# Row factors of two RMS norms sent to all partitions through DRAM instead of by a diagonal and a matrix product

## The chip, the cores and the metric

The kernel runs on one core of a Trainium2 chip. The metric is the device time of one execution in microseconds (us). The kernel before takes 1819.01 us, the median of three runs (1817.65 to 1820.26).

## The reference, cut to what matters

The program is one hybrid decoder layer in float32 and a last norm, on 2048 tokens of 1024 features.

```python
h = rms_norm(x, norm1_g)
proj = h @ w_in                                  # u_a, v_a, val_b, gate_b
a_out = spatial_gating(u_a, v_a, ...)            # within chunks of 128 tokens
b_out = conformer_conv(val_b, gate_b, ...)       # causal depthwise, 31 taps
x = x + concat([a_out, b_out]) @ w_out
h = rms_norm(x, norm2_g)                         # the second norm
f = square(relu(h @ w_ff1))
x = x + f @ w_ff2
return rms_norm(x, final_g)                      # the last norm

def rms_norm(x, g):
    return x * rsqrt(mean(x * x, axis=-1) + EPS) * g
```

Each norm needs one factor per token, r = rsqrt(mean of squares + EPS). The two norms that matter here are the second and the last.

## The kernel before, in words

Activations lie transposed: features on the 128 partitions, tokens along the row. The 2048 tokens are four blocks (b = 0 to 3) of 512; a tile of 128x512 holds 128 features of one block. A factor per token is therefore a factor per column, and must be the same on all 128 partitions before it can multiply a tile.

**How a factor comes about.** The squares of a block are added over the eight feature tiles (square_add), and feature_sums (L490) multiplies them by a column of ones, which gives the sum over partitions as a tile of 128x4: token 128n + p stands at partition p, column n (tile ssum). VectorE (DVE) computes ve, the mean plus EPS, and GpSimd (POOL) raises it to -1/2: r, 128x4.

**How r reaches all partitions before.** DVE multiplies an identity by r, which gives dg, four diagonals of 128x128; TensorE (PE) multiplies it by a matrix of ones, so that every partition of the PSUM tile rbc holds all 512 factors. The two matrices are plain fp32, and the trace shows two records for this one product. For the second norm ScalarE (ACT) copies the tile to SBUF, into r_rows (row_scale, L625). For the last norm of blocks 0 and 1 the tile rbc3 stays in PSUM and is read from there by eight products of DVE, one for each feature tile (finish, L1129).

**Precision.** Other products are made of three matmuls (mm3) on fp32r parts: high x high, low x high and high x low. ACT makes the high part and POOL, or DVE, the low one.

**The stages.** The input projections and the convolution come first. stage_o(b) (L647) is the output projection of block b; when its last tile is done, row_scale(b) is put on a list with a due time. later(n, f) (L598) runs f at the n-th following beat, and beat comes twice for each tile. The up multiply u0 serves blocks 0 and 1, u1 blocks 2 and 3, each as seven products over 2x2 blocks in place of eight; up_out (L978) multiplies each sum by r_rows on DVE (L992, recorded as c<-c,r_rows or c<-py,r_rows) and squares it. The down multiply has 16 chunks, numbered 0 to 15, eight for each pair of blocks. A chunk (down_chunk, L1242) has 28 steps, STEPS (L1084), each named (i, j): i is one of the seven products and j one of four tiles. A step is six matmuls into a tile py and one DVE addition from it to a residual tile x. Products 1, 5 and 2 open PSUM tiles; 6, 7 and 4 go on in the four tiles of product 1, and 3 goes on in those of product 5. So a step of product 3 has to wait until the addition that reads the same tile after product 5 is done. The steps begin (1,0) to (1,3), (5,0) to (5,2), (6,0) to (6,3), (3,0) to (3,2), (5,3). In the down phase there are eight PSUM banks for all of this, ssum and rbc3 included.

**The finishes.** Blocks 1 and 0 are complete in the last steps of chunk 7. finish(b) is a generator that goes one step on at each step of chunks 8 and 9, beside the matmuls: sums, r, gaps of so many steps, diagonal, product, and then one product of DVE and one store a step. Blocks 3 and 2 end the kernel; their finishes (finish_third, finish_last) are other functions and stay as they are.

**What sets the order.** Most of the program, the down phase but its last chunk included, is reordered by the framework's scheduler, which simulates a timeline. stage_o, the two up multiplies and the last chunk keep the order as written. Engines run their instructions in order, and wait by semaphores. SyncE (SP) issues nearly all DMAs in one order, and stands still while one of them waits.

Of the kernel before, what the change touches and what calls it, by code (L numbers as in the profile page):

```python
# [9 lines left out]
F32 = mybir.dt.float32  # L10
# [3 lines left out]
ALU = mybir.AluOpType  # L14

P = 128
# [3 lines left out]
TB = 512  # L20
KD = D // P
# [6 lines left out]
V_FG = 36  # L28
# [54 lines left out]
def hybrid_block_kernel(  # L83
# [14 lines left out]
    nc = tc.nc  # L98
    dve = Clocked(nc.vector, lambda n: 0.35 if n <= 128 else 0.17 + n / 960.0)
    dcv = Clocked(nc.vector, lambda n: 0.15 + n / 960.0, dve.clock)  # L100
    dsb = Clocked(nc.vector, lambda n: 0.22 + n / 512.0 if n <= 512 else n / 640.0, dve.clock)
    gps = Clocked(nc.gpsimd, lambda n: 0.35 + n / 488.0 if n > 8 else 1.1)
    pe = Clocked(nc.tensor, lambda n: 0.0135 + n / 2400.0)
    pe4 = Clocked(nc.tensor, lambda n: 0.0135 + n / 600.0, pe.clock)
# [3 lines left out]
    dram = ctx.enter_context(tc.tile_pool(name="dram", bufs=1, space=bass.MemoryType.DRAM))  # L108
# [17 lines left out]

    p_d = dram.tile([2, 4, P, 2, TB], F32, name="p_d")
    x1_d = dram.tile([NB, 4, P, 1024], F32, name="x1_d")
    f_d = [dram.tile([8, 4, P, 2, TB], F32, name=f"f_d{i}") for i in range(2)]
    w2_d = dram.tile([8, 7, 2, P, 2, 512], F32, name="w2_d")  # L130
    w1_d = dram.tile([2, 7, P, 2, 512], F32, name="w1_d")
# [8 lines left out]
    def tmp(name, dtype=F32):  # L140
        return t2.tile([P, 512], dtype, tag="tmp", name=name)

    def bank(kind, name):
        return banks[kind].tile([P, 512], F32, tag=kind, name=name)

    def mm_tile(name):
        return bank("mm", name)

    def tp_tile(name):
        return bank("tp", name)  # L150

    def tiny(name, n=4):
        return small.tile([P, n], F32, tag=f"{name}{n}", name=name)
# [9 lines left out]
    def rest(src, hi, lo):  # L163
        n = src.shape[1]
        for e in (gps, dsb):
            e.time = max(e.time, pe.time - 8.0)
        e = gps if gps.time < max(pe.time + GPS_LEAD[0], dsb.time - 2.0) else dsb
        e.tensor_tensor(lo, src, hi.bitcast(F32), op=ALU.subtract)
# [67 lines left out]
    ones = const.tile([P, P], F32, name="ones")  # L236
# [12 lines left out]
    def v(off, j):  # L249
        return vec[:, off + j:off + j + 1]  # L250

    def rsqrt(dst, src, mul):
        n = dst.shape[1]
        ve = tiny("ve")
        dve.tensor_scalar(ve[:, :n], src, mul, EPS, op0=ALU.mult, op1=ALU.add)
        gps.tensor_tensor(dst, ve[:, :n], nhalf.to_broadcast([P, n]), op=ALU.pow)
# [167 lines left out]
    def spread(r, ps):  # L424

        dg = tmp("dg")
        n = r.shape[1]
        dsb.tensor_tensor(
            dg.rearrange("p (n t) -> p n t", t=P)[:, :n, :],
            ident.unsqueeze(1).to_broadcast([P, n, P]),  # L430
            r.unsqueeze(2).to_broadcast([P, n, P]), op=ALU.mult)
        yield
        pe4.matmul(ps, ones, dg[:, :n * P], start=True, stop=True)
# [56 lines left out]
    def feature_sums(acc, n, pc=None):  # L490

        pc = tp_tile("ssum") if pc is None else pc
        for i in range(n):
            for k, sq in enumerate(acc):
                pe4.matmul(pc[:, i:i + 1], sq[:, i * P:(i + 1) * P], ones[:, 0:1],
                           start=k == 0, stop=k == len(acc) - 1)
        return pc[:, :n]
# [100 lines left out]
    def later(n, f, first=False):  # L598
        due.append([n, f, first])
# [22 lines left out]
    def w_lo(n):  # L622
        rest(raws[n], *loaded[n])

    def row_scale(b):  # L625

        r = r2[b]

        def spread_out():
            ps = tp_tile("rbc")  # L630
            g = spread(r, ps)
            next(g)

            def product():
                next(g, 0)
                later(1, lambda: nc.scalar.copy(r_rows[:, b % 2, :], ps))
            later(1, product)

        def sums():
            ps = feature_sums(acc[b], 4)  # L640
            later(1, lambda: rsqrt(r, ps, 1.0 / D))
            later(2, spread_out)
        return sums

    r_rows = const.tile([P, 2, TB], F32, name="r_rows")

    def stage_o(b, at):  # L647
        def evict(d, ps):
            def square():
                square_add(acc[b], xr[b][d])  # L650
                if d == KD - 1:
                    later(2, row_scale(b))

            def go():
                dve.tensor_tensor(xr[b][d], ps, xr[b][d], op=ALU.add)
                later(1, square)
                if d % 2:
                    later(1, lambda: nc.sync.dma_start(x1_d[b, d // 2], xt1[b][d // 2]))
                at(d)
            return go  # L660
# [25 lines left out]
    for kp in range(1, 4):  # L686
# [10 lines left out]
        out=wt, in_=wt, pattern=[[0, 4], [1, P]], compare_op=ALU.is_ge, fill=0.0,  # L697
# [52 lines left out]
    late, _ = stage_v(1, h[1], parts[1])  # L750
# [4 lines left out]
    late, _ = stage_v(2, h[2], parts[2])  # L755
# [9 lines left out]
    late, _ = stage_v(3, h[3], parts[3])  # L765
# [212 lines left out]
    def up_out(pair):  # L978
        kept = {}

        def out(m, i, ps):
            blk_ = INTO[i]
            def copy():
                kept[m, blk_] = tmp("c")
                nc.scalar.copy(kept[m, blk_], ps)  # L985

            def finish():
                if i == 4:
                    src, c = ps, tmp("c")
                else:  # L990
                    c = kept.pop((m, blk_))
                    src = c if i == 7 else ps  # L992
                    dve.tensor_tensor(src, ps, c, op=ALU.add)
                (dsb if i == 7 else dve).scalar_tensor_tensor(
                    c, src, 0.0, r_rows[:, blk_[1], :], op0=ALU.max, op1=ALU.mult)
                later(1, lambda: nc.scalar.activation(c, c, AF.Square))  # L996
                later(2, lambda: nc.scalar.dma_start(
                    f_d[pair][m // 2, 2 * blk_[0] + blk_[1], :, m % 2, :], c))

            later(1, copy if i in (1, 5, 6) else finish, True)  # L1000
        return out
# [65 lines left out]
    with tc.manual_schedule():  # L1067
        stage_o(2, at_o2)
        pace["w2"] = 0.0
        k = w2st.at[2]  # L1070
# [4 lines left out]
    dn = {"x": [[] for _ in range(NB)]}  # L1075
# [53 lines left out]
    def finish(b, acc):  # L1129

        gaps = (6, 3, 4)
        for _ in range(gaps[0]):
            yield
        r = tiny("r1")
        ve = tiny("ve")
        ps = feature_sums(acc, 4, mm_tile("ssum"))
        yield
        dve.tensor_scalar(ve, ps, 1.0 / D, EPS, op0=ALU.mult, op1=ALU.add)
        gps.tensor_tensor(r, ve, nhalf.to_broadcast([P, 4]), op=ALU.pow)
        for _ in range(gaps[1]):  # L1140
            yield
        dg = tmp("dg")
        times_ident(dg, r)
        for _ in range(gaps[2]):
            yield
        ps = mm_tile("rbc3")
        pe4.matmul(ps, ones, dg, start=True, stop=True)
        x = dn["x"][b]
        for k in range(KD):
            yield  # L1150
            dve.scalar_tensor_tensor(x[k], x[k], v(V_FG, k), ps, op0=ALU.mult, op1=ALU.mult)
            nc.sync.dma_start(out[b, k // 2, :, k % 2, :], x[k])

    def times_ident(dg, r):
        dsb.tensor_tensor(
            dg.rearrange("p (n t) -> p n t", t=P), ident.unsqueeze(1).to_broadcast([P, 4, P]),
            r.unsqueeze(2).to_broadcast([P, 4, P]), op=ALU.mult)

    def gained(x, ks):
        for k in ks:  # L1160
            nc.scalar.activation(x[k], x[k], AF.Copy, scale=v(V_FG, k))
# [232 lines left out]
```

## Time and profile before

| | |
|---|---|
| median of three runs | 1819.01 us |
| the profiled execution | 1819.57 us |
| its span in the trace | 1817.8 us |
| granted TensorE clock, mean | 0.998 |
| PE busy | 1805.2 us (99%) |
| DVE busy | 1318.6 us (73%) |
| POOL busy | 1232.4 us (68%) |
| ACT busy | 754.6 us (42%) |
| DMA moved | 424.74 MB, mean 234 GB/s |

The span is the time that the trace covers; the execution's own time is 1.8 us longer. A timeline row gives start, duration, engine, line, operation, output tile <- inputs, shape and count, and in brackets how long the engine stood idle before it and for whom. SPq is SP issuing a DMA. A row of a table of groups ends with busy time in us, mean ns of one, and idle time before. A row of the table of waits reads: engine and instruction, what it waited for, us in total, times, longest. In the chain of waits a row is a start, a duration and what held the end at that time. Line 78 is the helper that records most instructions, so tiles, not lines, tell them apart.

### The profile page before, as it was taken

How to read it: one execution, taken by the hardware profiler on the slowest of the kernel's cores; microseconds unless marked ns; L12 is line 12 of the kernel's file. 1: busy time of each engine (PE TensorE's matmuls, PEld its weight loads, DVE VectorE, ACT ScalarE, POOL GpSimd, SP SyncE). 2: the span in 40 equal slices, each digit the busy share in tenths (PEclk: the TensorE clock that was granted, in tenths of full speed). 3: DMA queues.
4: the chain of work that ended last, by engine and by line, in shares of the span. 5: the costliest groups of instructions: out<-in, count | busy, mean ns of one | idle time of the engine just before them, and what ended most of it. 6: DMA issues, size and time to landing. Idle time of an engine off the chain costs nothing.

```text
span 1817.8 us, 23247 instructions
## 1 busy us (share of the span) xinstructions
PE 1805.2 (99%) x8080; PEld 1488.0 (82%) x8080; DVE 1318.6 (73%) x1832; ACT 754.6 (42%) x1170; POOL 1232.4 (68%) x788
## 2 busy tenths in 40 slices
PE   9999999999999999999999999999999999999998
PEld 7888888888888888888888888888888887888886
DVE  4699997996898985532667787787766678665565
ACT  6435556454454454455455555433212131222112
POOL 4575986884766666699778989786756464444434
PEclk9999999999999999999999999999999999999999
DMA  8353637442645464685557778999987679777752
GB/s 337 107 173 101 222 135 272 163 145 81 231 152 180 161 215 179 224 298 207 189 191 276 271 255 298 354 401 382 357 350 262 255 259 336 297 240 259 254 185 93
DMA packets 131686, 424.74 MB, mean 234 GB/s; under 512 B 14576, under 2 KB 15216, under 8 KB 131568
## 3 DMA queue, kind: packets, MB, share of 16 engines
q1 hardware_dynamic: 96000, 329.12, 50.7%
q10 hardware_dynamic: 35568, 94.13, 13.2%
q8 instruction: 64, 1.05, 0.2%
q14 instruction: 54, 0.44, 0.1%
HBM read 302.60 MB, written 120.59 MB: 233 GB/s over the span
## 4 chain that ended last, share of the span: by engine, by line
PE 92%; DVE 6%; issue 1%; POOL 1%; DMA 0%; ACT 0%; POOLq 0%; SPq 0%; DVEq 0%; ACTq 0%
PE py L78 51%; PE pz L78 9%; PE po L78 9%; PE px L78 5%; PE pv L78 4%; PE pg L78 4%; PE pu L78 4%; PE pvv L78 4%; DVE acc L78 3%; PE sgu L78 1%; PE rbc L78 0%; PE ssum L78 0%; DMA raw<-in_w_o 0%; PE cb L78 0%; PE ct L78 0%
## 5 line engine op out<-in xcount | busy, mean ns | idle before, releaser
L78 PE MATMUL py<-fo_hi,w2o 128*128 128x512 f32 x1792 | 555.1, 390 | 1.0 <-DVE x L78 1.0
L78 POOL TENSOR_TENSOR fo_lo<-fraw,fo_hi 128x1024 fp32r<-128x1024 f32 x112 | 283.0, 2535 | 260.6 <-ACT fo_hi L160 231.1
L78 DVE TENSOR_TENSOR x<-py,x 128x512 f32<-128x512 f32 x448 | 299.9, 687 | 175.4 <-PE py L78 175.2
L78 PEld LDWEIGHTS py<-fo_hi,w2o 128*128 128x128 f32 x1792 | 336.4, 188 | 71.6 <-DVE x L78 1.4
L78 PE MATMUL py<-hop,w1o 128*128 128x512 f32 x1536 | 363.6, 390 | 0.5 <-ACT c L985 0.5
L78 PE MATMUL py<-fo_lo,w2o 128*128 128x512 f32 x896 | 348.6, 389 | 0.0
L78 PEld LDWEIGHTS py<-hop,w1o 128*128 128x128 f32 x1536 | 287.7, 188 | 62.0 <-issue 1.3
L78 DVE SCALAR_TENSOR_TENSOR acc<-g,vec,acc 128x512 f32<-128x512 f32 x464 | 324.4, 750 | 1.9
L160 ACT CAST fo_hi<-fraw 128x1024 fp32r<-128x1024 f32 x112 | 116.9, 1052 | 424.7 <-PE py L78 209.7
L78 POOL TENSOR_TENSOR w_lo<-raw,w_hi 128x1024 fp32r<-128x1024 f32 (+1 forms) x94 | 224.1, 2390 | 61.4 <-ACT w_hi L160 50.9
L78 POOL TENSOR_TENSOR w1o<-wraw,w1o 128x512 fp32r<-128x512 f32 x120 | 172.9, 1446 | 51.9 <-ACT w1o L813 42.0
L78 PEld LDWEIGHTS py<-fo_lo,w2o 128*128 128x128 f32 x896 | 168.2, 188 | 35.6 <-issue 0.7
L78 PE MATMUL pz<-hop,w1o 128*128 128x512 f32 x768 | 183.8, 390 | 0.0
L78 POOL TENSOR_TENSOR w1o<-ws,w1o 128x512 fp32r<-128x512 f32 x90 | 128.9, 1435 | 65.4 <-ACT w1o L813 60.3
L78 PEld LDWEIGHTS pz<-hop,w1o 128*128 128x128 f32 x768 | 143.8, 188 | 29.7
L78 DVE TENSOR_TENSOR fraw<-fraw 128x1024 f32<-128x1024 f32 x64 | 92.1, 1439 | 16.3 <-POOL fo_lo L78 14.3
L996 ACT ACTIVATE c<-c 128x512 f32<-128x512 f32 x128 | 80.8, 632 | 54.8 <-DVE c L78 54.2
L78 PE MATMUL po<-m_hi,w_hi 128*128 128x512 f32 x256 | 101.1, 395 | 0.0
L78 PE MATMUL po<-m_hi,w_lo 128*128 128x512 f32 x256 | 99.9, 390 | 0.6 <-POOL w_lo L78 0.6
L78 PE MATMUL po<-m_lo,w_hi 128*128 128x512 f32 x256 | 99.7, 389 | 0.0
L78 DVE TENSOR_TENSOR px<-px,c 128x512 f32<-128x512 f32 x32 | 22.4, 699 | 102.3 <-PE px L78 69.0
L78 POOL TENSOR_TENSOR w2p<-wraw,w2p 128x512 fp32r<-128x512 f32 x64 | 92.6, 1447 | 2.6 <-ACT w2p L813 2.6
(157 smaller groups left out, 2928.4 us busy)
## 6 DMA issues: line engine op xcount, KB each, us to landing
w2o<-w_d SPq DMA_DIRECT2D x224, 512.0 KB, 6.2
w_d<-w2p ACTq DMA_DIRECT2D x112, 512.0 KB, 5.0
wraw<-in_w SPq DMA_DIRECT2D x92, 512.0 KB, 4.6
f_d<-c ACTq DMA_DIRECT2D x128, 256.0 KB, 4.0
fraw<-f_d SPq DMA_DIRECT2D x64, 512.0 KB, 6.7
raw<-in_w_ct SPq DMA_DIRECT2D x48, 512.0 KB, 5.2
raw<-in_w_o SPq DMA_DIRECT2D x32, 512.0 KB, 5.9
w1o<-w_d SPq DMA_DIRECT2D x28, 512.0 KB, 5.5
```

The source lines that it names most:

```text
L78: return op(out, *args, **kwargs)
L160: nc.scalar.copy(hi, src)
L996: later(1, lambda: nc.scalar.activation(c, c, AF.Square))
```

## The change

**The second norm, all four blocks.** The diagonal (DVE), the product (PE) and the copy to r_rows (ACT) are gone. In their place r is stored to a DRAM tensor r_d at the second beat after the sums (write_factor: 128x4, 512 elements of 4 bytes that each go to a place of their own, since the order of r in DRAM is token by token), and read from there into r_rows at the fourth beat, the 2 KB row to all 128 partitions (read_factor, 256 KB). Both DMAs are on SP, and the read waits for the write.

**The last norm of blocks 0 and 1.** The diagonal, the product and its PSUM bank are gone. In their place: the write, ACT's product of tiles x[0] and x[2] with the gain (gained), three steps later the read into an SBUF tile rows, and four steps later the products: POOL multiplies x[0] and x[2] by rows, DVE the six others by gain and rows. Each store stands two steps behind its product.

The core of the diff:

```diff
     def row_scale(b):
         r = r2[b]
-        def spread_out():
-            ps = tp_tile("rbc")
-            g = spread(r, ps)
-            next(g)
-            def product():
-                next(g, 0)
-                later(1, lambda: nc.scalar.copy(r_rows[:, b % 2, :], ps))
-            later(1, product)
         def sums():
             ps = feature_sums(acc[b], 4)
             later(1, lambda: rsqrt(r, ps, 1.0 / D))
-            later(2, spread_out)
+            later(2, lambda: write_factor(b, r))
+            later(4, lambda: read_factor(b, r_rows[:, b % 2, :]))
+    r_d = dram.tile([6, 4, P], F32, name="r_d")
+    def write_factor(n, r):
+        nc.sync.dma_start(r_d[n].rearrange("n p -> p n"), r)
+    def read_factor(n, rows):
+        nc.sync.dma_start(rows, r_d[n].rearrange("n p -> (n p)").unsqueeze(0).to_broadcast([P, TB]))
     def finish(b, acc):
...
-        dg = tmp("dg")
-        times_ident(dg, r)
+        write_factor(4 + b, r)
+        gained(dn["x"][b], (0,2))
+        for _ in range(gaps[1]):
+            yield
+        rows = tmp("rows")
+        read_factor(4 + b, rows)
         for _ in range(gaps[2]):
             yield
-        ps = mm_tile("rbc3")
-        pe4.matmul(ps, ones, dg, start=True, stop=True)
         x = dn["x"][b]
-        for k in range(KD):
+        for k in range(KD + 2):
             yield
-            dve.scalar_tensor_tensor(x[k], x[k], v(V_FG, k), ps, op0=ALU.mult, op1=ALU.mult)
-            nc.sync.dma_start(out[b, k // 2, :, k % 2, :], x[k])
+            if k in (0,2):
+                gps.tensor_tensor(x[k], x[k], rows, op=ALU.mult)
+            elif k < KD:
+                dve.scalar_tensor_tensor(
+                    x[k], x[k], v(V_FG, k), rows, op0=ALU.mult, op1=ALU.mult)
+            if k > 1:
+                nc.sync.dma_start(out[b, k // 2 - 1, :, k % 2, :], x[k - 2])
```

**How it moves instructions.** Three places show it, all at the finish of block 1 in chunk 8. First SP before: x loads (x1_d, L1079), weight loads of the down phase (w2o, L1119), and the stores of the finished block (out, L1152).

```order
L1119 DMA w2o<-w_d 128x1024 x2
L1079 DMA x_12888<-x_d 128x1024
L1119 DMA w2o<-w_d 128x1024 x2
L1152 DMA out<-x_10182 128x512
L1111 DMA fraw<-f_d_87 128x1024
```

And SP now; r_d is the DRAM tensor of factors, rows the SBUF tile that is read back.

```order
L1119 DMA w2o<-w_d 128x1024 x2
L628 DMA r_d<-r_12830 128x4x1
L1079 DMA x_12877<-x_d 128x1024
L632 DMA rows<-r_d 128x512
L1119 DMA w2o<-w_d 128x1024 x2
L1159 DMA out<-x_10171 128x512
L1159 DMA out<-x_10216 128x512
L1111 DMA fraw<-f_d_88 128x1024
```

The write stands behind a pair of weight loads, an x load stands between write and read, and the next pair of weight loads stands behind the read.

Second, DVE before, at the same place: additions of steps (1,3) and (5,0), the eight products, the addition of (5,1).

```order
L78 TENSOR_TENSOR x_12829<-py,x_12829 128x512
L78 TENSOR_TENSOR x_12586<-py,x_12586 128x512
L78 SCALAR_TENSOR_TENSOR x_10182<-x_10182,vec,rbc_12941 128x512 x2
L78 SCALAR_TENSOR_TENSOR x_10227<-x_10227,vec,rbc_12941 128x512 x2
L78 SCALAR_TENSOR_TENSOR x_10269<-x_10269,vec,rbc_12941 128x512 x2
L78 SCALAR_TENSOR_TENSOR x_10307<-x_10307,vec,rbc_12941 128x512 x2
L78 TENSOR_TENSOR x_12656<-py,x_12656 128x512
```

And DVE now:

```order
L78 TENSOR_TENSOR x_12818<-py,x_12818 128x512
L78 TENSOR_TENSOR x_12575<-py,x_12575 128x512
L78 SCALAR_TENSOR_TENSOR x_10171<-x_10171,vec,rows 128x512
L78 SCALAR_TENSOR_TENSOR x_10216<-x_10216,vec,rows 128x512
L78 SCALAR_TENSOR_TENSOR x_10258<-x_10258,vec,rows 128x512 x2
L78 SCALAR_TENSOR_TENSOR x_10296<-x_10296,vec,rows 128x512 x2
L78 TENSOR_TENSOR x_12645<-py,x_12645 128x512
```

The run of products stays between the same two additions; it has six instead of eight, and reads rows instead of rbc.

Third, PE before, after step (3,0): py_13038 is the tile of (5,3), py_12943 that of (5,1), into which (3,1) adds. In brackets the engines for which an instruction waits.

```order
L78 MATMUL py_12933<-fo_hi_12771,w2o_12769 128x512
L78 MATMUL py_13038<-fo_hi_12699,w2o_12695 128x512 [waits DVE_49]
L78 MATMUL py_13038<-fo_lo_12700,w2o_12695 128x512
L78 MATMUL py_13038<-fo_hi_12699,w2o_12695 128x512
L78 MATMUL py_13038<-fo_hi_12699,w2o_12697 128x512
L78 MATMUL py_13038<-fo_lo_12700,w2o_12697 128x512
L78 MATMUL py_12943<-fo_hi_12771,w2o_12767 128x512 [waits DVE_49]
```

And PE now, where py_13020 is the tile of (5,3) and py_12933 that of (5,1):

```order
L78 MATMUL py_12925<-fo_hi_12760,w2o_12758 128x512
L78 MATMUL py_13020<-fo_hi_12688,w2o_12684 128x512
L78 MATMUL py_13020<-fo_lo_12689,w2o_12684 128x512
L78 MATMUL py_12933<-fo_hi_12760,w2o_12756 128x512 [waits DVE_49]
L78 MATMUL py_12933<-fo_lo_12761,w2o_12756 128x512
```

The new tile of (5,3) no longer waits for DVE, and two of its matmuls instead of five stand ahead of (3,1), which does.

Of block 0's finish: its sums stood before in two pieces, after steps 19 and 20 of chunk 8, and stand now in one piece, 16 matmuls ahead of the end of that chunk. Its run of products on DVE stands between the additions of (1,3) and (5,0) of chunk 9; on SP the write follows twelve of the next fourteen weight loads, and the read follows two more.

## The prediction

> **What bounds the kernel now.** I read the page first, for the engine that sets the end.
>
> ```profile
> span 1817.8 us, 23247 instructions
> PE 1805.2 (99%) x8080; PEld 1488.0 (82%) x8080; DVE 1318.6 (73%) x1832; ACT 754.6 (42%) x1170; POOL 1232.4 (68%) x788
> ```
>
> TensorE (PE) is busy for 1805.2 of 1817.8 us. The time is therefore the sum of PE's work, and a change gains what it takes out of PE's stream or out of the few places where PE stands still. The table of waits of PE lists those places:
>
> ```profile
> PE first L245 <- DVE idle L242: 1.7, 1, 1.7
> PE py L78 <- DVE x L78: 1.0, 1, 1.0
> ...
> PE rbc L78 <- DVE dg L78: 0.2, 1, 0.2
> ```
>
> The last two belong to the change: both lie in the last norm of block 1, the finish that runs inside the down phase. Everything else that the change touches is work of PE itself, or work beside it.
>
> **What one product costs PE.** The timeline of PE at block 0's second norm shows a diagonal's product between ordinary matmuls:
>
> ```profile
> 382.62 0.40 PE L78 MATMUL pu<-h_hi,w_hi 128*128 128x512 f32 x1
> 382.86 1.02 PE L78 MATMUL rbc<-dg,ones 128*128 128x512 f32 x2
> 383.31 0.80 PE L78 MATMUL pu<-h_lo,w_hi 128*128 128x512 f32 x1
> ```
> ```profile
> 496.54 0.86 PE rbc L78 x2
> 497.40 8.21 PE py L78 x36
> ```
>
> Matmuls follow each other at 8.21/36 = 0.228 us; the fp32 product (two records) holds PE for 0.86 us (the last two rows are from the chain of waits, at block 1's second norm). Nothing runs on PE beside it, so **each removed product is worth 0.86 us**, with no wait around these four. Term 1: 4 blocks x 0.86 = **3.44 us**. The diagonal on DVE and the copy on ACT go too, but neither engine bounds the time: I count them at nothing.
>
> What must hold for term 1 is that the factors arrive in time by DRAM. The tightest use is block 1's, in the timelines of POOL and DVE:
>
> ```profile
> 491.45 1.02 POOL L78 TENSOR_TENSOR r<-ve,nhalf 128x4 f32<-128x4 f32 x1 [1.36 <-DVE ve L78]
> ```
> ```profile
> 503.80 1.21 DVE L78 SCALAR_TENSOR_TENSOR c<-c,r_rows 128x512 f32<-128x512 f32 x1
> ```
>
> From 492.47 to 503.80 there are 11.3 us for write and read. If the two need more, DVE stands there by the excess, once, and PE behind it. SP is held as well while it waits for r and for the write: behind it stand one or two weight loads, each issued several tiles ahead of use. I price that at nothing; a load that came late would cost its lateness, once.
>
> **Finish of block 1, before.** The timeline gives the whole story:
>
> ```profile
> 1492.85 1.02 POOL L78 TENSOR_TENSOR r<-ve,nhalf 128x4 f32<-128x4 f32 x1
> ```
> ```profile
> 1496.28 0.39 PE L78 MATMUL py<-fo_hi,w2o 128*128 128x512 f32 x1
> 1496.85 1.13 PE L78 MATMUL rbc<-dg,ones 128*128 128x512 f32 x2 [0.17 <-DVE dg L78]
> ...
> 1498.04 0.39 PE L78 MATMUL py<-fo_lo,w2o 128*128 128x512 f32 x1
> 1507.14 0.39 PE L78 MATMUL py<-fo_hi,w2o 128*128 128x512 f32 x1
> 1508.49 0.50 PE L78 MATMUL py<-fo_hi,w2o 128*128 128x512 f32 x1 [0.97 <-DVE x L78]
> ```
> ```profile
> 1503.10 5.34 DVE L78 SCALAR_TENSOR_TENSOR x<-x,vec,rbc 128x512 f32<-128x512 f32 x8
> 1508.36 4.87 DVE L78 TENSOR_TENSOR x<-py,x 128x512 f32<-128x512 f32 x8
> ```
>
> The product costs 1498.04 - 1496.28 less two steps of 0.228, that is 1.31 us (with its 0.17 wait). Then PE stops: 1508.49 - 1507.14 - 0.23 = 1.12 us. It restarts 0.05 us after the eighth product on DVE ends (1503.10 + 5.34 = 1508.44). What starts there is the first matmul into a fresh PSUM tile, that of (5,3); seven of the eight banks hold live sums and the eighth is rbc3, which those products read. So the stop is the rbc3 bank. Product and stop together are 2.43 us, all that finish 1 can give.
>
> **Finish of block 1, after.** The bank is free, so (5,3) no longer waits. But the next wait stands right behind: two matmuls of (5,3) later comes (3,1), which adds into the bank of (5,1), and the DVE addition of (5,1) is queued behind the six products, which now wait for the rows out of DRAM. Call L the time from r ready (1492.85 + 1.02 = 1493.87) to rows landed, and R the time of DVE's run of six. (3,1) can start one addition (4.87/8 = 0.61) after that run: at 1493.87 + L + R + 0.65. Without a stop PE would be there at 1507.14 + 0.23 - 1.31 + 2 x 0.23 = 1506.5. So **term 2 = 2.43 - max(0, L + R - 12.0)**.
>
> L has no row of its own: no DMA here writes 4-byte pieces. The nearest rows, by issue on SP and by landing:
>
> ```profile
> 1492.08 0.86 SPq L1119 DMA_DIRECT2D w2o<-w_d  x2
> DMA to landing us min/median/max: 4.4/4.9/5.5
> ...
> DMA to landing us min/median/max: 3.5/4.2/5.0
> ...
> DMA to landing us min/median/max: 2.0/2.9/9.3
> ...
> DMA to landing us min/median/max: 2.6/5.0/9.5
> ```
>
> They are, in turn: two weight loads that stand just ahead of the write on SP, their landing, that of the x loads of the same stretch, that of all stores and loads of p_d, that of the loads of hf (256 KB, as the new read). Bounds: 2.0 + 2.6 = 4.6 us to 9.3 + 9.5 = 18.8 us. For the write I take 5.0: the second weight load, issued near 1492.5, lands near 1497.5, and the write, 2 KB in 512 pieces, cannot land much before it. For the read I take 3.4, just under the shortest x load, which moves twice its bytes: SP has few transfers out there. **L = 8.4** (an estimate). The Trainium skill (DMA: Bandwidth & Descriptors, Rules for kernel authors) says that a non-contiguous last dimension lowers to one descriptor per element, and its Specifications that below 512 B the DMA does read-modify-write; this speaks against the write, and no run here shows its price.
>
> R: before, eight products from PSUM took 5.34, 0.67 each; now both tensors of a product lie in SBUF while POOL does its two products. The groups by shape:
>
> ```profile
> L78 DVE SCALAR_TENSOR_TENSOR c<-c,r_rows 128x512 f32<-128x512 f32 x32 | 33.3, 1040 | 1.3
> L78 DVE SCALAR_TENSOR_TENSOR xr<-xr,vec 128x512 f32<-128x512 f32 x24 | 28.6, 1207 | 25.3 <-POOL hop L78 25.0
> L78 DVE SCALAR_TENSOR_TENSOR c<-px,r_rows 128x512 f32<-128x512 f32 x32 | 22.1, 692 | 1.1
> L78 POOL TENSOR_TENSOR x<-x,rows 128x512 f32<-128x512 f32 x4 | 5.0, 1271 | 4.8 <-ACT rows L1233 4.6 <-ACT rows L1185 0.2
> ```
>
> With one operand in PSUM an operation takes 692 ns, with both in SBUF 1040 or 1207. Bounds for six: 6 x 0.67 = 4.0 to 6 x 1.207 = 7.2; POOL's two last 2.5 us and are over before the run ends, so I take 4.0 plus most of them, **R = 6.0**. The Trainium skill (SBUF — State Buffer, Who interferes with whom) has this as a rule: a DVE instruction with two SBUF inputs contends with a GpSimd one that reads SBUF, with at most one it does not; in its Terms the loser fully blocks. The rows above agree, 692 against 1040; by full blocking R would be 4.0 + 2.5 = 6.5, and my sum 1.0 us smaller, 1815.8.
>
> With L = 8.4, R = 6.0: term 2 = 2.43 - 2.4 = **0.0**. The product's time comes back as a longer stop at (3,1).
>
> **Finish of block 0.** Its product costs 0.88 in the timeline of PE:
>
> ```profile
> 1531.14 0.40 PE L78 MATMUL py<-fo_hi,w2o 128*128 128x512 f32 x1
> 1531.38 1.02 PE L78 MATMUL rbc<-dg,ones 128*128 128x512 f32 x2
> ...
> 1532.47 0.40 PE L78 MATMUL py<-fo_lo,w2o 128*128 128x512 f32 x1
> ```
> ```profile
> 1520.04 0.50 PE L78 MATMUL ssum<-ones,sq 128*128 128x1 f32 x4
> ```
> ```profile
> 1525.89 1.01 POOL L78 TENSOR_TENSOR r<-ve,nhalf 128x4 f32<-128x4 f32 x1
> ```
>
> (1532.47 - 1531.14 - 2 x 0.228 = 0.87.) After, the sums stand 16 matmuls ahead of chunk 9's start C, so they end at C - 3.6. Before, r was ready 6.4 us after the sums, with POOL busy; at the least ve and r need 1.2. I put r at C (between C - 2.4 and C + 2.8). Here the six products stand between the additions of (1,3) and (5,0); (3,0) waits for the latter, 66 matmuls after C, or 15.0 us. Term 3 = 0.87 - max(0, L + R + 0.65 - 15.0) = 0.87 - 0.05 = **0.8**. The SP rows ahead (next weight loads) are issued before the write ends. POOL's splits behind its two products serve chunk 10, over 20 us away; the stores, two steps on, have no reader.
>
> **Sum.** 3.44 + 0.0 + 0.8 = 4.2 us. The profiled run took 1819.57 (span 1817.8 and 1.8 around it), the median of the three is 1819.01, 0.56 less; 1819.57 - 4.2 = 1815.4, and by the median **1814.8 us**.
>
> With R = 6.0 the gain is 6.7 for L up to 6.0; 12.7 - L up to 8.3; and 21.0 - 2L above, where both finishes stop PE. It falls under 3.6 us (0.2%, about what a measurement of this kernel can tell from no change) at L = 8.7, to nothing at 10.5, and is -3.6 at 12.3. One more us of R counts like one of L.
>
> **Rivals.**
> - *Both stops vanish* (L at most 7): 5.7 to 6.7 us less, down to 1812.3. For it: stores land in 2.0 at the least. Against it: the loads ahead on the queue land near 1497.5. Chance 0.16.
> - *The stops give the products' time back* (L between 8.7 and 12.3): 1815.4 to 1822.6, near 1817 at L = 9.5. For it: write and read follow one another, and loads of 256 KB have a median of 5.0. Against it: the up-phase saving is untouched by it. Chance 0.34.
> - *Slower: the write is slow.* 512 pieces of 4 B take as long as the slowest DMAs: with 9.3 for it and 3.4 for the read L is 12.7, DVE stands with both queues of additions behind it, and the time is 1819.0 + 4.4 = 1823.4; from L = 12.3 on it is slower by over 0.2%. With 18.8 it would be 1835.6, and block 1's rows would be late too. For it: 512 separate pieces, and no row shows such a store. Against it: 2 KB, and p_d's stores of 256 KB land in 2.0 at the least. Chance 0.11. (The Trainium skill's rule on one descriptor per element, above, would bring this case; no run here shows it.)
>
> **How the numbers follow.** The forecast, L from 7 to 8.7 (1813.3 to 1815.4), has 0.39. Faster by over 0.2%: 0.39 + 0.16 = 0.55; within: 0.34; slower: 0.11. The range leaves out the slow write and the upper part of the second rival (L over 10.5, about 0.08): 1812.2 to 1819.0.
>
> **What would show it.** Right: six products fewer on PE, no wait at the rows' first uses in the up phase, and in chunk 8 a wait of PE of some 2.4 us for DVE's x at (3,1), with rows landing some 8 us after r. Write and read landing apart show which estimate failed; six products on DVE longer than 6 us show R. A wait of DVE for r_rows in the up phase, or a gap at chunk 9's (3,0) of over 1 us, would make the forecast wrong, as would an r_d write that lands 9 us after issue.

## The result and the profile after

The changed kernel takes 1841.99 us (median of four runs, 1839.94 to 1843.60) against 1819.06 us (four runs) before: ratio 1.0126, 95% interval 1.0114 to 1.0139. It is 23 us slower, where 4.2 less was forecast. The profiled execution took 1839.94 us.

The head of the page after, to be read against the same lines of before:

```profile
span 1838.2 us, 23249 instructions
PE 1804.6 (98%) x8068; PEld 1487.5 (81%) x8068; DVE 1315.9 (72%) x1823; ACT 754.9 (41%) x1170; POOL 1237.0 (67%) x791
```

PE's busy time fell by 0.6 us, and its idle time grew from 1817.8 - 1805.2 = 12.6 to 1838.2 - 1804.6 = 33.6 us. The 21.0 us of new idle time, less those 0.6, are the 20.4 us between the spans. (Busy time fell by so little, with six products gone, in part because it also holds a slower clock, shown below.) The table of waits of PE says where the idle time lies:

```profile
PE py L78 <- DVE x L78: 9.3, 1, 9.3
PE py L78 <- issue: 8.3, 1, 8.3
PE py L78 <- POOL hop L78: 1.9, 3, 0.9
...
PE ct L78 <- DVE c L78: 1.7, 1, 1.7
...
PE py L78 <- ACT hop L946: 0.9, 2, 0.5
```

Before there was one wait of 1.0 us here. The first two rows are one stop each in chunks 8 and 9; the last three, 4.5 us in all, belong to the up phase, where rows of the second norm come late. The chain of waits after shows what stood ahead of the two stops:

```profile
1495.14 1.03 POOL r L78
1496.17 0.02 issue
1496.18 9.68 DMA r_d<-r
...
1505.94 5.28 DMA rows<-r_d
...
1513.02 5.01 DVE x L78 x6
1518.02 0.04 issue
1518.07 19.79 PE py L78 x78
...
1542.80 8.45 DMA r_d<-r
```

The 2 KB write took 9.68 us and the read 5.28, then DVE's run of six and one addition held PE until 1518.07. The same chain shows a write of 8.45 us at block 0's finish. DVE's own rows, its two runs of six, with the wait ahead of each:

```profile
1511.24 6.17 DVE L78 SCALAR_TENSOR_TENSOR x<-x,vec,rows 128x512 f32<-128x512 f32 x6 [6.96 <-DMA rows<-r_d]
...
1557.22 8.26 DVE L78 SCALAR_TENSOR_TENSOR x<-x,vec,rows 128x512 f32<-128x512 f32 x6 [8.62 <-DMA rows<-r_d]
```

For the second stop the profile names no releaser ("issue"), but it ends as the first does, one addition after the run of six: 1557.22 + 8.26 = 1565.48, some 0.6 for the addition, and PE goes on at 1566.19.

```profile
1566.19 0.77 PE L78 MATMUL py<-fo_hi,w2o 128*128 128x512 f32 x1 [8.34 <-issue]
```

A table by stretch adds one cost that no wait shows. Its columns are the stretch, its length, PE's busy time and matmuls, granted clock (1.00 is full speed), DMA share and GB/s:

```profile
1514.00:1518.00 4.00, 0.00 (x0) 0.50 0.77 208
1518.00:1522.00 4.00, 3.93 (x9) 0.51 1.04 401
1522.00:1526.00 4.00, 4.00 (x19) 1.00 1.06 324
```

While PE stands, its granted clock falls to 0.50, and for about 4 us after the stop PE runs at half speed: 9 matmuls where 19 would fit. The chain has the price: 78 matmuls in 19.79 us, where 0.228 each makes 17.8, so about 2.0 us for this stop. In the changed kernel's timeline 31 matmuls after the other stop took 8.95 us, about 1.9 more than 31 x 0.228.

### The profile page after: what moved, and what is told of

It reads as the page before. It is cut to its first block, busy times and chain, and to the rows that moved or that the text cites. A ratio compares the mean times of both kernels' runs of the same rounds, so it can differ in the third digit from the quotient of the medians.

```text
span 1838.2 us, 23249 instructions
## 1 busy us (share of the span) xinstructions
PE 1804.6 (98%) x8068; PEld 1487.5 (81%) x8068; DVE 1315.9 (72%) x1823; ACT 754.9 (41%) x1170; POOL 1237.0 (67%) x791
## 4 chain that ended last, share of the span: by engine, by line
PE 88%; DVE 6%; DMA 3%; issue 2%; POOL 1%; ACT 0%; POOLq 0%; SPq 0%; DVEq 0%; ACTq 0%
PE py L78 49%; PE po L78 9%; PE pz L78 9%; PE px L78 4%; PE pv L78 4%; PE pg L78 4%; PE pu L78 4%; PE pvv L78 4%; DVE acc L78 3%; DMA r_d<-r 1%; PE sgu L78 1%; PE ssum L78 0%; DMA fraw<-f_d 0%; POOL hop L78 0%; DVE c L78 0%
## 5 line engine op out<-in xcount | busy, mean ns | idle before, releaser
L78 DVE TENSOR_TENSOR fraw<-fraw 128x1024 f32<-128x1024 f32 x64 | 96.3, 1505 | 13.1 <-POOL fo_lo L78 10.7
L78 POOL TENSOR_TENSOR hop<-xr,hop 128x512 fp32r<-128x512 f32 x55 | 75.0, 1381 | 27.3 <-ACT hop L946 20.2
```

The lines of the kernel that those rows point to most:

```text
L78: return op(out, *args, **kwargs)
```

## The experiments

**The two halves apart.** finish_alone puts row_scale back as it was before; norm2_alone puts finish back.

```diff
@@ finish_alone, row_scale
-            later(2, lambda: write_factor(b, r))
-            later(4, lambda: read_factor(b, r_rows[:, b % 2, :]))
+            later(2, spread_out)
@@ norm2_alone, finish
-        write_factor(4 + b, r)
-        read_factor(4 + b, rows)
+        times_ident(dg, r)
+        pe4.matmul(ps, ones, dg, start=True, stop=True)
```

> Only the last norm's half of the change (blocks 0 and 1); the second norm keeps its diagonal, product and copy. Theory (slow write, waited for in the down phase): the two stops of PE, 9.3 and 8.3 us in the changed kernel's trace, and about 2.0 us after each at a lower clock, less the 3.3 us that the removed products and the old stop cost: about +18 us, 1837. Rival (the second norm's half costs most, since its four factors come late): within 5 us of the kernel before, at most 1824.

> Only the second norm's half of the change; the finishes are those of before. Theory: 3.4 us saved on PE, and about 4.5 us of waits of PE that follow the late rows of blocks 1 and 3: near +1 us, 1820, with DVE waiting some 5 us twice for r_rows. Rival (this half costs most): 1832 or more.

finish_alone: 1839.99 us, ratio 1.0117 (1.0102 to 1.0133), with stops of PE of 12.4 and 8.7 us. The longer stop follows a longer write: issued at 1493.7, read at 1505.8, 12.1 us. norm2_alone: 1822.22, ratio 1.0017 (1.0008 to 1.0026). So the finishes cost about 21 us and the second norm about 3.4; together 24.5, near the 23 of the whole. The second norm's half was 2 us worse than expected; its table by stretch shows that late rows cost there too, in idle time and in clock. The middle row is a piece of the first:

```profile
480.00:530.00 50.00, 48.34 (x208) 0.97 0.56 198
...
514.00:516.00 2.00, 2.00 (x6) 0.50 0.95 326
...
910.00:960.00 50.00, 47.67 (x201) 0.97 0.58 213
```

The idle time is 1.7 and 2.3 us and the clock takes some 1.5 us in each stretch: 7.0 us, less the 3.4 saved, is 3.6 against the measured 3.4. In the first stretch the clock fell to half behind three waits of 0.3 to 0.9 us within 3 us, with only three matmuls between them.

**Is the write slow, or the queue ahead of it?** write16 stores r as it lies, 128 pieces of 16 B, and its products read rows through a turned view; write_act leaves the 512 pieces and issues them on ScalarE's queue. Both have the second norm of before.

```diff
@@ write16
-        nc.sync.dma_start(r_d[n].rearrange("n p -> p n"), r)
+        nc.sync.dma_start(r_d[n], r)
@@ write_act
-        nc.sync.dma_start(r_d[n].rearrange("n p -> p n"), r)
+        nc.scalar.dma_start(r_d[n].rearrange("n p -> p n"), r)
```

> As finish_alone, but r is stored in the order in which it lies, 128 pieces of 16 B instead of 512 of 4 B, and the products read the row through a turned view. Theory (the write takes about 9 us because of its 512 pieces): write of 3 to 5 us, stops of PE of 3 to 5 us each instead of 9.3 and 8.3, time 1823 to 1829. Rival (the write is short and stands behind the weight loads on its queue): write and time as in finish_alone, 1837. Second rival (the products get slower by the turned view): DVE's run of six above 8 us.

> As finish_alone, but the write is issued on ScalarE's queue instead of SP's, past the weight loads. Theory (512 pieces): write of 8 to 9 us as before, time 1837. Rival (queue): write of 2 to 4 us, the rows land some 6 us earlier, stops of PE of about 3 us, time 1822 to 1826.

write_act: 1841.73 us, and the rows for its waits read

```profile
SPq L632 <- DMA r_d<-r: 18.0, 2, 10.1
```

SP, which issues the read, still stood about 9 us for each write, with the weight loads on the other queue: the write's place behind them on SP is not what makes it slow. write16: 1828.79, ratio 1.0054 (1.0038 to 1.0071). Its timelines of SP show the write's length as the time from its issue to that of the read, which waits for it:

```profile
1493.90 0.32 SPq L628 DMA_DIRECT2D r_d<-r  x1
...
1499.34 0.32 SPq L632 DMA_DIRECT2D rows<-r_d  x1
...
1539.56 0.32 SPq L628 DMA_DIRECT2D r_d<-r  x1
...
1542.03 0.32 SPq L632 DMA_DIRECT2D rows<-r_d  x1
```

5.4 and 2.5 us instead of 9.7 and 8.5. PE's stop was 8.8 us in chunk 8 and 1.1 in chunk 9, not the 3 to 5 of the expectation, since the second rival held as well: through the turned view the run of six took 8.93 and 9.05 us. Most single products took 1.11 us there, against 0.74 in the changed kernel.

**Sums token by token.** norm2_16 and finish_16 let the sums read every fourth column of the squares, so that r lies token by token, the store has 16-byte pieces and the products read rows straight.

```diff
-                pe4.matmul(pc[:, i:i + 1], sq[:, i * P:(i + 1) * P], ones[:, 0:1],
+                pe4.matmul(pc[:, i:i + 1], sq.rearrange("q (p n) -> q n p", n=4)[:, i, :] if by4
+                           else sq[:, i * P:(i + 1) * P], ones[:, 0:1],
```

> As norm2_alone, but the sums are taken from every fourth column, so that r lies token by token and its store has 128 pieces of 16 B. Theory (pieces): write 2.5 to 5.5 us instead of 7 to 9, DVE's waits for r_rows (6.1, 5.5 and 4.3 us) gone or under 1 us, time 1815.5 to 1817.5. Rival (the read, or the order of the work, is what is late): 1820 or more.

> As finish_alone, with the sums from every fourth column and a store of 128 pieces; the products read rows straight. Theory, by the formula of the prediction with the L of write16 (11.8 and 7.4) and the R of finish_alone (6.2 and 8.3): a stop of 6.0 us at (3,1) of chunk 8, 1.4 us or less in chunk 9, time 1822 to 1825, against 1828.8 of write16. Rival (the turned view was not what made R 8.9 there): stop near 8.8 us, time as write16.

finish_16: 1824.68 (ratio 1.0030, 1.0019 to 1.0041), a stop of 5.8 us at (3,1), near the 6.0 expected, and the run of six took 6.2 us. norm2_16: 1818.28 (ratio 1.0000, 0.9990 to 1.0009). DVE no longer waits for r_rows at all, but the 3.4 us of the four products did not appear. The timeline of PE shows where they went, first in norm2_16, then before:

```profile
357.97 1.80 PE L78 MATMUL ssum<-ones,sq 128*128 128x1 f32 x8
```

```profile
358.25 0.95 PE L78 MATMUL ssum<-ones,sq 128*128 128x1 f32 x8
```

Eight sums with a strided stationary operand take 0.85 us more, as much as a product. I had not priced that.

**Squares in turned order.** norm2_turned leaves the sums as they were and lets ScalarE write the squares in that order.

```diff
-        nc.scalar.activation(sq, src, AF.Square)
+        if turn:
+            nc.scalar.activation(sq.rearrange("q (n p) -> q n p", p=P),
+                                 src.rearrange("q (p n) -> q n p", n=4), AF.Square)
+        else:
+            nc.scalar.activation(sq, src, AF.Square)
```

> As norm2_16, but not the sums read every fourth column: ScalarE writes the squares in that order, so that the sums' matmuls read them straight, and r is token by token with a store of 128 pieces. Theory (in norm2_16 the eight sums of a block took 1.64 us on PE instead of 0.79, which ate the saving of 0.86 a block): no wait for r_rows, sums back at 0.8 us, and the 3.4 us of the four products left as a gain: 1815.2. Rival (the saving was lost elsewhere): 1818 to 1819 as norm2_16.

1815.99 us, ratio 0.9983 (0.9974 to 0.9992), so 1.5 to 4.7 us faster than before. Write and read now follow one another on SP at once:

```profile
367.83 0.33 SPq L632 DMA_DIRECT2D r_d<-r  x1
369.23 0.33 SPq L636 DMA_DIRECT2D r_rows<-r_d  x1
```

1.4 us, where the changed kernel has 8.3 at the same place (366.83 to 375.11). PE has no idle time between 480 and 530 us or between 910 and 960. So term 1 of the prediction is there when the rows come in time, and this version, which keeps the finishes of before, has the lowest median of all kernels here. The price lies on ScalarE, which is not the bottleneck: a turned square takes 1.13 us instead of 0.63.

**Products held back.** held is finish_alone with the products made to wait for a later step, so that nobody stands for the rows. both_16_held and both_turned_held have both halves of the change, 16-byte stores (the first by strided sums, the second by turned squares), and the same holding back.

```diff
-        for _ in range(gaps[2]):
+        for _ in range(gaps[2] + 12):
             yield
+        one = tiny("ve")[:, :1]
+        dve.tensor_scalar(one, latest[0][:, :1], 0.0, 1.0, op0=ALU.mult, op1=ALU.add)
+        nc.scalar.activation(rows, rows, AF.Copy, scale=one)
```

> As finish_alone (512 pieces, second norm as before), but the products are held back: rows is copied in place on ScalarE by a factor of one that is computed from a residual tile some twelve steps later, so that the products come after the landing. Theory (the loss is DVE's stand in front of its queue of additions and PE's behind it): both stops vanish, the write may stay at 9 us, and what is left is the saving of the products and of the old stop, 3.3 us: 1815.5. Rival (the DMAs themselves disturb, SP standing 9 us with weight loads behind it, or DVE and GpSimd contending): 1822 or more, with PE waiting for w2o or fo_lo.

> Both halves of the change, all stores with 128 pieces, the finishes' products held back as in held. Theory: no product is left but those of blocks 2 and 3's ends, no stop of PE of over 1 us in chunks 8 and 9, time 1818.9 - 3.4 - 3.3, so 1812 to 1814. Rival (the up phase gives its saving back by waits for r_rows): 1815 to 1817.

> As both_16_held with the squares in turned order, sums read straight. Theory: 1819.7 less six times 0.85 us: 1814.5, which would beat the kernel before by 4 us. Rival: as norm2_turned's; 1818 or more.

held: 1825.97 (ratio 1.0043, 1.0027 to 1.0059), 14 us better than finish_alone but 10 worse than expected. Neither theory alone covers it. DVE no longer waits for rows, but PE stops twice, for 1.7 and 6.1 us. The timeline of DVE ahead of the longer stop:

```profile
1519.34 1.23 DVE L78 TENSOR_TENSOR fraw<-fraw 128x1024 f32<-128x1024 f32 x1 [6.27 <-POOL fo_lo L78]
...
1526.82 9.31 DVE L78 SCALAR_TENSOR_TENSOR x<-x,vec,rows 128x512 f32<-128x512 f32 x6
```

The products now run beside POOL's splits and take 9.3 us, and the next chunk's operands (fraw) come late, behind an SP that stood for the write, here 13.2 us. With the short write the stop is 2.0 us (both_16_held, 1819.67, ratio 1.0008, 0.9999 to 1.0018; its six strided sums cost the 5.1 us of six products). both_turned_held: 1817.05, ratio 0.9989 (0.9980 to 0.9998), against 1814.5 expected; PE still stops 2.3 us in chunk 8. So finishes through DRAM did not beat the finishes of before, held back or not: norm2_turned, which keeps those, is 1 us faster in the median, and the runs of the two overlap.

**Stores by themselves.** probe adds stores and reads that nobody waits for to the kernel before, in chunks 10 to 14; probe_stores adds five kinds of stores in the up phase.

```diff
+            d = probe_d[2 * m + (i == 7)]
+            nc.sync.dma_start(
+                d.rearrange("n p -> p n") if i == 6
+                else d.rearrange("n p -> (n p)").rearrange("(p n) -> p n", n=4), r)
...
+            nc.sync.dma_start(t, sgu_b.rearrange("n p -> (n p)").unsqueeze(0).to_broadcast([P, TB])
+                              if i == 2 else xt[m % NB, 0, :, 0, :])
```

> The kernel before, with DMAs added that nobody waits for, one each in five chunks of blocks 2 and 3: a store of a 128x4 tile as 512 pieces of 4 B, the same as 128 pieces of 16 B, a read of one 2 KB row to all partitions, and a plain load of 256 KB. Theory (pieces): 512 pieces land in 8 to 10 us, 128 pieces in 2 to 5, both reads in 5 to 6, the time within 2 us of before. Rival (the store is slow only where the finish puts it): both stores alike. Second rival (the broadcast is slow because all pieces come from one row): plain load under 4 us beside 5 to 6.

> The kernel before, with five more stores of r (128x4) after each block's second norm, that nobody waits for: four, 512 pieces of 4 B as in the change (neighbouring partitions side by side in DRAM); row, 128 pieces of 16 B; pairs, 512 pieces of 4 B that lie 8 B apart, each partition's own four together; one, 128 pieces of 4 B; apart, 512 pieces of 4 B that lie 64 B apart. Theory (the number of pieces): four, pairs and apart 8 us or more, row and one 1.4 to 3 us where the queue is short. Rival (neighbouring partitions' pieces share a line of DRAM): four and one slow, pairs and apart 1.4 to 4 us. Second rival (4 B is what is slow, not the number): one 5 us or more. The time within 3 us of before.

probe: 1818.58, ratio 0.9998 (0.9988 to 1.0008); these DMAs by themselves cost nothing that the runs can tell. The 512 pieces landed in 10.0 to 12.4 us, the 128 in 7.6 to 8.8: among the loads of those chunks the medians are 2.1 us apart, and neither case of the expectation for the stores held. The two reads, by tile, the broadcast first:

```profile
DMA to landing us min/median/max: 5.9/6.4/6.9
...
DMA to landing us min/median/max: 3.6/8.5/9.0
```

The broadcast read is not slower than a plain load there, and never short. probe_stores (one run, 1819.38 us) spoke against my theory of the number of pieces: 128 adjacent pieces of 4 B (one) landed in 8.2 to 10.9 us, 512 pieces 64 B apart in 4.6 to 5.8 and once in 12.4. But each kind stood at another place among the loads, and even the 16-byte pieces (row) took 5.6 to 12.6 us there.

So place_a, place_b and place_c put the kinds at the places of the change's own stores, moved on by one block from kernel to kernel, and place_d two more. (One run each, 1818.2 to 1819.8 us, all within 1.3 us of the kernel before.)

```diff
             later(2, spread_out)
+            kinds = [(one_d[b], r[:, :1]), (pairs_d[b, :, :, 0], r), (apart_d[b, :, :, 0], r)]
+            to, of = kinds[(b + 0) % 3]               # + 1 in place_b, + 2 in place_c
+            later(2, lambda: nc.sync.dma_start(to, of))
```

> The kernel before with one more store of r after each block's second norm, at the place where the change has its store, with no reader; blocks 0 to 3: one (128 pieces of 4 B, adjacent), pairs (512 pieces of 4 B, 8 B apart, each partition's four together), apart (512 pieces, 64 B apart), one. If the number of pieces makes the store slow: one 1.4 to 3 us, pairs and apart 8 to 9. If it is adjacent 4-byte pieces of different partitions: one 7 us or more, pairs and apart 1.5 to 5 us.

> As place_a with the kinds moved on: pairs, apart, one, pairs for blocks 0 to 3. If the number of pieces: one 1.4 to 3, pairs and apart 8 to 9. If adjacent pieces: one 7 or more, pairs and apart 1.5 to 5 us.

> As place_a with the kinds moved on: apart, one, pairs, apart for blocks 0 to 3. If the number of pieces: one 1.4 to 3, pairs and apart 8 to 9. If adjacent pieces: one 7 or more, pairs and apart 1.5 to 5 us.

> The same places: lone (128 pieces of 4 B, 64 B apart) at blocks 0 and 2, eight (128 pieces of 8 B, adjacent) at blocks 1 and 3. If adjacent small pieces of different partitions are slow: lone 1.4 to 3 us, eight between the 1.4 of 16 B and the 8 of 4 B. If 4 B by itself is slow: lone 7 or more.

The landings by the traces, from issue to landing, in us:

| store of r | pieces | blocks 0, 1, 2, 3 |
|---|---|---|
| as in the change (after) | 512 of 4 B, neighbours side by side | 8.3, 8.7, not recorded, 8.9 |
| one | 128 of 4 B, side by side | 7.5, 9.6, 8.4, 7.0 |
| pairs | 512 of 4 B, 8 B apart, by partition | 3.8, 4.8, 4.4, 3.8 |
| apart | 512 of 4 B, 64 B apart | 3.0, 2.9, 3.6, 3.5 |
| eight | 128 of 8 B, side by side | 3.2 and 3.4 (blocks 1, 3) |
| lone | 128 of 4 B, 64 B apart | 1.4 and 1.6 (blocks 0, 2) |
| norm2_turned | 128 of 16 B, side by side | 1.4, 1.4, 1.4, 1.4 |

The rows of one and apart at the same place, block 0, from place_a and place_c:

```profile
L648 SPq DMA_DIRECT2D one_d<-r x1: 326/326/326, 366.8 to 366.8; - x1
...
DMA to landing us min/median/max: 7.5/7.5/7.5
```

```profile
L648 SPq DMA_DIRECT2D apart_d<-r x1: 600/600/600, 367.5 to 367.5; - x1
...
DMA to landing us min/median/max: 3.0/3.0/3.0
```

128 pieces take 7.0 to 9.6 us when 4 bytes of neighbouring partitions lie side by side in DRAM and 1.5 when each has 64 B to itself; four times as many pieces, apart, take 3.3. At these places the number of pieces costs some 2 us; the side-by-side placing of the 4-byte pieces costs most of the rest. What inside the memory makes it so, the runs do not show. At the finishes only the 16-byte store was tried, not the pieces kept apart.

## Why the prediction was wrong

*What bounds the kernel*: right. The end moved by PE's idle time and clock.

*Term 1, 3.44 us for four products*: right in its price (norm2_turned gains 2.7 in all, 1.5 to 4.7 by its interval). Wrong was to count on the 11.3 us as enough for block 1's write and read. They took 8.7 and about 6.5, and DVE stood at the first use. The timeline of DVE after:

```profile
506.70 0.69 DVE L78 SCALAR_TENSOR_TENSOR c<-c,r_rows 128x512 f32<-128x512 f32 x1 [5.10 <-DMA r_rows<-r_d]
```

A second wait of the kind is at block 3. By the table by stretch of the changed kernel this left PE 3.0 us idle between 480 and 530 us and 1.5 between 910 and 960, which takes term 1 back and 1.1 us more.

*The formula of term 2*: right. With the measured L = 1511.24 - 1496.17 = 15.1 and R = 6.2 it gives a stop of 15.1 + 6.2 - 12.0 = 9.3 us, and the trace has 9.3. For write16 it gives 8.7 (L 11.8, R 8.9), where the trace has 8.8; for finish_alone 12.3 (L 18.1, R 6.2), where it has 12.4. That the bank of rbc3 made the old stop and that (3,1) makes the new one is borne out. *Term 3* holds too: L = 14.4, R = 8.3, 22.7 - 14.3 = 8.4 against 8.3. For write16 it is 1 us too high, 2.1 (L 7.4, R 9.05) against 1.1.

*L = 8.4*: this is the step that failed. The write was put at 5.0 us and took 9.7 and 8.5; the read was put at 3.4 and took 5.3 and 5.9. The write was reckoned from the loads ahead of it, as if its own part were nothing; the nearest rows were all of long pieces. At the second norm, with a short queue, the same store alone took 8.3 us where 16-byte pieces took 1.4. Why the read takes 5 to 7 us, no run settles: it was no shorter in norm2_turned (5.1 to 7.1). The bounds, 4.6 to 18.8, did hold the measured 15.1 and 14.4, and the rival with the slow write named the mechanism; I gave it 0.11, and its mark of 12.3, from which the kernel is slower by over 0.2%, was passed at both finishes. The signs that the prediction named for being wrong all came: DVE waited for r_rows, PE stood 8.3 us in chunk 9, and the write landed after 9.7 us. The Trainium skill (DMA: Bandwidth & Descriptors, Rules for kernel authors) warned of one descriptor per element for such a store. The store was slow, but the runs put the number of pieces second: 512 pieces 64 B apart land in 2.9 to 3.6 us.

*R = 6.0*: 6.2 at block 1, 8.3 at block 0, where a split of POOL's ran beside it; in held 9.3. All beyond the eight products from PSUM, 5.3. The prediction took 1040 ns as what a product with both tensors in SBUF costs. That is a mean of unlike ones. The rows of the tiles r_rows before and rows after (block 1) give shortest, median and longest in ns:

```profile
L78 DVE SCALAR_TENSOR_TENSOR c<-c,r_rows x32: 691/694/2708, 503.8 to 1174.2; 128x512 f32<-128x512 f32 x32
...
L78 DVE SCALAR_TENSOR_TENSOR x<-x,vec,rows x6: 739/740/1851, 1511.2 to 1516.7; 128x512 f32<-128x512 f32 x6
```

The median, 694, is that of a product with an operand in PSUM (691). Of the six products two took 1.85 and 1.75 us, just while POOL did its two, and four 0.74.

*What was left out*: the clock. Each of the two stops cost about 2 us more at half clock. The Trainium skill (TensorE: Matmul & The Clock Gate, What's actually happening) has the granted clock fall to half after an idle window of about 3.4 us and come back after as long a busy one; the rows agree, 0.50 in the stop and 0.51 in the 4 us behind it. In norm2_alone, though, the clock fell to 0.50 with no single wait there longer than 1.0 us; the measurement decides, so short waits close together did it too.

The sum with measured values: 3.44 - 4.5 (up phase), term 2 2.43 - 9.3 = -6.9, term 3 0.87 - 8.4 = -7.5, clock -3.9: 19.4 us slower, 1839.0 against the profiled 1839.94. The profiled execution is the fastest of the four, and the median is 2 us above it; that is not explained. Against the forecast the sum is 23.6 us off: 12.7 by L (some 8.2 by the writes, 4.4 by the reads), 4.5 by the late rows of the up phase, 3.9 by the clock and 2.5 by R.

## What to carry to other kernels

A round trip through DRAM has to be reckoned with its own landing times in both directions, here 7 to 18 us in all, and compared with the time to the first use, not with the engine time that it saves. A wait placed in front of a shared in-order queue costs every item behind it: six products that nobody needed held up the additions that PE needed. Where a small vector has to go out, let each partition write its 16 B in one piece (1.4 us here against 8.3 to 8.9), or keep the partitions' pieces apart (64 B apart, 1.4 to 3.6). A mean over a group can hide two kinds of instruction: read the median and the longest too.

## What the runs showed of the hardware that I had not expected

- 128 stores of 4 B from neighbouring partitions into adjacent words: 7.0 to 9.6 us. The same 64 B apart: 1.4 and 1.6. In 8-byte pieces 3.2 and 3.4, in 16-byte pieces 1.4.
- A sum by PE whose stationary operand is read at a stride of 16 B: 1.80 us for eight, against 0.95 with adjacent columns.
- A product on DVE that reads a tile through a turned view: 1.11 us against 0.74 straight. A run of six, with POOL's two products beside it, took 8.9 and 9.1 us against 6.2.
- A stop of PE of 8 to 9 us costs some 2 us on top of itself, by the clock; the 12.4 us stop of finish_alone about 2.8 (0.50 over 3.4 busy us, then 0.73 over 4.0). In norm2_alone three waits of at most 1.0 us close together cost some 1.5 by the clock, twice.
